# The price list of a work planner: charging VectorE and ScalarE by the times that the profile shows for one instruction

## The chip, the core and the metric

The kernel runs on one core of a Trainium2 chip. A core has a matrix engine (TensorE, PE in the profile, whose weight loads are listed as PEld), a vector engine (VectorE, DVE), an engine for activation functions (ScalarE, ACT), a general engine that here only issues DMAs and clears memory (GpSimd, POOL), and a queue engine that issues DMAs (SyncE, SP). Each has its own instruction stream and waits for the others by semaphores. SBUF is the on-chip memory, PSUM the accumulators that TensorE writes; a kernel keeps its data in tiles of 128 partitions, and tiles of one tag share a fixed number of buffers.

The metric is the device time of one execution in microseconds, as the median over runs.

## The reference

One layer of a diffusion backbone. `x` holds 256 latent tokens of width 2048, `ctx` 256 context tokens; everything is float32.

```python
sh1_x, sc1_x, g1_x, sh2_x, sc2_x, g2_x = adaln(c, w_mod, b_mod)       # silu(c) @ w_mod + b_mod, six parts; the same for c_ctx
hx = rmsnorm(x, norm1_g) * (1 + sc1_x) + sh1_x                         # hc from ctx in the same way
zx = hx @ w_in + b_in;  zc = hc @ w_in + b_in
s5 = s5_mixer(zc[:, 0:512], zx[:, 0:512], ...)          # diagonal complex state space, 32 groups x 64 states, both directions
cv = conv_module(zx[:, 512:1536], ...)                  # gate, depthwise convolution of 31 taps, layer norm, silu
ml = mlstm_mixer(zc, zx, ml_norm_g)                     # 4 heads of 256, both directions, chunkwise linear attention
x = x + g1_x * (concat([s5, cv, ml]) @ w_out)
x = x + g2_x * swiglu(rmsnorm(x, norm2_g) * (1 + sc2_x) + sh2_x, w_ffn_in, w_ffn_out)   # hidden width 5632
return rmsnorm(x, norm_f_g)
```

## The kernel before, in words

**The weight stream.** All large weight matrices are cut into 128x128 tiles and packed by `tile_order()` into one stream of 386 chunks of 8 tiles (`wst`), in the order in which they are used. A chunk is loaded by one DMA of 512 KB on SyncE's queue (`raw`, three buffers), rounded to the short float32 format on ScalarE (`whi`, line 201, `acopy`), and the rest `raw - whi` is taken on VectorE (`wlo`, line 168, `tt`). Every product is then formed from two or three matmuls of these parts. `nxt()` hands out the next weight tile; at the first tile of a chunk it starts the load and the split of a chunk ahead, and then calls `sc.pump()`.

**The stages**, in the order in which their weights lie in the stream: the first sixteen rows of tiles, with part of the K projection and the S5 input (chunks 0 to 13); the convolution's input (14 to 29); the rest of K (30 to 39); V (40 to 55); Q (56 to 71); the output gate O (72 to 87); the S5 gate GLU (88, 89); the first half of the output projection (90 to 105), which needs the convolution and S5; its second half (106 to 121), which needs the attention; and the feed-forward network (122 to 385), in four blocks.

**Side jobs.** Everything that is no weight matmul of these stages is written as a Python generator that yields between short pieces, and is registered with a planner, `Sched`, under a priority (lower goes first): `gates_job` (1), `mod_job` (2), `conv_job` and `s5_job` (3), `attention` (4). `mod_job` computes the four later parts of the modulation vector: the first (q = 0) by matmuls on TensorE, the others (q = 1, 2, 3) as sixteen steps a block of 512 columns, one on ScalarE and fifteen `scalar_tensor_tensor` on VectorE (`macc`, 128x512), followed by four transposes; four blocks make a q, eight loads `wm` of 512 KB a block come through GpSimd's queue with four buffers, and a step of four such instructions asks to be called again 10,000 units of TensorE time later (6,400 while on TensorE). `s5_job` works through 16 pairs of state groups; `prep` of the next pair runs beside `main5` of this one, and copies and a split (`gT`, `gs`) end it. `conv_job` takes the four channel tiles as their inputs come (`cdone`), 31 `scalar_tensor_tensor` each (`XB`, 128x256), then a layer norm. `attention` is registered at the start of stage Q and does the four heads one after the other; `qh` has one buffer, the state tiles `RH` one for each direction.

**The account.** `Sched` keeps three running sums in nanoseconds, `pe`, `dve` and `act`. Each helper that issues an instruction adds its price: `mm` (line 203) adds for a matmul of n columns `max(n, 256) / 2.36` (four times that for full float32), the helpers at lines 167 to 200 add for VectorE and ScalarE. These sums are Python numbers; they set only in which order instructions are emitted. `pump()` is called once a chunk and lets in pieces of ready jobs, the lowest priority number first and the earliest due among equals, until an engine's sum is more than `AHEAD` before TensorE's:

```python
def pump(self):
    self.dve = max(self.dve, self.pe - LAG)
    self.act = max(self.act, self.pe - LAG)
    for _ in range(400):
        if self.dve > self.pe + AHEAD or self.act > self.pe + AHEAD:
            return
        ready = [j for j in self.jobs if j[2] <= self.pe]
```

with `AHEAD, LAG = 3500.0, 500.0`. Where a later stage needs a job's result, `finish(j)` (or `need_mod(q)`) emits all that is left of it at once, without the pump: `conv_job` and `gates_job` at the start of V (lines 1019, 1020), `s5_job` and `attention` after O, ahead of GLU, `readout` and `need_mod(2)` between the halves of the output projection (the feed-forward input is scaled by these vectors, `A2` and `mods[:, 1]`).

The framework below then gives each engine its instructions in about this order of emission; where the inputs of an instruction are late in its own plan of times, it can put a later one first.

Of the kernel before, what the change touches and what calls it, by code (L numbers as in the profile page):

```python
# [36 lines left out]
MOD_PACE_D = 5000.0  # L37
P_CONV, P_S5, P_MOD, P_ATT, P_GATE = (3, 3, 2, 4, 1)
AHEAD, LAG = 3500.0, 500.0
PUMP_EVERY = 8  # L40
S5_Y = (3000, 0, 0, 0)
ATT_Y = (200, 1200, 3000)
# [108 lines left out]
def hybrid_layer_kernel(ctx: ExitStack, tc: tile.TileContext, xt, ctxt, wm1, wmr, wst, wg, bvrow, pvd, cstd, s5p, out):  # L151
# [6 lines left out]
    sc = Sched()  # L158


    def n_of(ap):
        n = 1
        for s in ap.shape[1:]:
            n *= s
        return n

    def tt(o, a, b, op):
        V.tensor_tensor(out=o, in0=a, in1=b, op=op)  # L168
        sc.dve += 62 + 1.05 * n_of(o)

    def ts(o, a, s1, op0, s2=None, op1=None):
        if op1 is None:
            V.tensor_scalar(o, a, s1, None, op0=op0)
        else:
            V.tensor_scalar(o, a, s1, s2, op0=op0, op1=op1)
        sc.dve += 62 + 0.6 * n_of(o)

    def stt(o, a, s, b, op0, op1):
        V.scalar_tensor_tensor(o, a, s, b, op0=op0, op1=op1)  # L179
        sc.dve += 62 + 1.05 * n_of(o)  # L180

    def vcopy(o, a):
        V.tensor_copy(o, a)
        sc.dve += 62 + 0.8 * n_of(o)

    def rsum(o, a):
        V.tensor_reduce(out=o, in_=a, op=OP.add, axis=mybir.AxisListType.X)
        sc.dve += 62 + 1.05 * n_of(a)

    def scan(o, d0, d1, init, op0, op1):  # L190
        V.tensor_tensor_scan(o, d0, d1, init, op0=op0, op1=op1)  # L191
        sc.dve += 62 + 1.05 * n_of(o)

    def act(o, a, f, bias=0.0, scale=1.0, pin=False):
        i = S.activation(o, a, f, bias=bias, scale=scale)  # L195
        if pin:
            tc.keep_in_program_order(i)
        sc.act += 190 + 0.84 * n_of(o)

    def acopy(o, a):  # L200
        S.copy(o, a)  # L201
# [61 lines left out]
    def split(c):  # L263
        his[c] = sb.tile([128, CH * 128], F32R, name="whi", tag="whi", bufs=3)
        acopy(his[c], raw[c])
        los[c] = sb.tile([128, CH * 128], F32R, name="wlo", tag="wlo", bufs=3)
        tt(los[c], raw[c], his[c], OP.subtract)
        for d in (raw, his, los):
            d.pop(c - 4, None)
# [6 lines left out]
    def split_to(c):  # L276
        while st["split"] <= min(c, NCH - 1):
            split(st["split"])
            st["split"] += 1

    def nxt(n=1):
# [3 lines left out]
        if i == 0:  # L285
# [4 lines left out]
            else:  # L290
                fetch_to(c + RAW_LA)
                split_to(c + SPL_LA)
        if i % PUMP_EVERY == 0:
            sc.pump()
# [18 lines left out]
    def rsqrt(o, ps, n, scale, eps, epsv):  # L313

        y, t = tmp(n), tmp(n)
        act(y, ps, AF.Ln, bias=eps, scale=scale)
        act(y, y, AF.Exp, scale=-0.5)
        stt(t, y, -0.5 * scale, y, OP.mult, OP.mult)
        stt(t, ps, epsv / scale, t, OP.add, OP.mult)
        stt(o, t, 1.5, y, OP.add, OP.mult)  # L320
# [28 lines left out]
    def load_gates():  # L349
        wgr = tmp(256).rearrange("p (k n) -> p k n", k=KT)  # L350
        nc.sync.dma_start(wgr, wg)
        acopy(wgs[:, :, 0:16], wgr)
        tt(wgs[:, :, 16:32], wgr, wgs[:, :, 0:16], OP.subtract)
# [22 lines left out]
    cs = sb.tile([128, KT, 32], F32, name="cs")  # L376
    V.memset(cs, 0.0)
    act(cs[:, :, 0], pvc("c", 0, 16), AF.Silu)
    act(cs[:, :, 1], pvc("cc", 0, 16), AF.Silu)
    b1sc = sb.tile([128, 16], F32, name="b1sc")  # L380
    ts(b1sc, pvc("bm", 16, 16), 1.0, OP.add)

    hx = sb.tile([128, KT, 2, NT], F32R, name="hx", tag="hx")
# [14 lines left out]
    def matvec_end(ft):  # L398
        ps = mvp.pop(ft)
        e = tmp(256)  # L400
        acopy(e, ps[:, 0:256])
        for i in range(2):
            P.transpose(ps[:, 256 + 128 * i:384 + 128 * i], e[:, 128 * i:128 * i + 128], ident)
        sc.pe += 220
        a = sb.tile([128, 4], F32, name="as1", tag="as1", bufs=4)
        rsum(a.rearrange("p (q r) -> p q r", q=2), ps[:, 256:512].rearrange("p (q j r) -> p q r j", q=2, j=4)[:, :, 0:2, :])
        ts(a[:, 0:2], a[:, 0:2], pvc("bm", ft), OP.add)
        ts(a[:, 2:4], a[:, 2:4], b1sc[:, ft:ft + 1], OP.add, pvc("n1g", ft), OP.mult)
        AS[ft] = a
# [3 lines left out]
    for half, src in ((0, xr), (1, cr)):  # L413
        for q in range(4):
            sq, s2 = tmp(), tmp()
            for i, t in ((0, sq), (1, s2)):
                act(t, src[:, 4 * q + 2 * i:4 * q + 2 * i + 2, :].rearrange("p k n -> p (k n)"), AF.Square)
            tt(sq, sq, s2, OP.add)
            for i in range(2):
                mm(stp[:, half * 256:half * 256 + 256], ones, sq[:, 256 * i:256 * i + 256], q + i == 0, q + i == 4,  # L420
                   native=True)
# [303 lines left out]
    def mod_job():  # L725
      for q in range(4):
        while mst["go"] < q:
            yield 500
        for b in range(4):
# [27 lines left out]
            if on_pe:  # L757
                rsum(dst, ps.rearrange("p (f j r) -> p f j r", f=4, j=4)[:, :, :, 0])
            else:
                for j in range(4):  # L760
                    S.activation(acc[:, 128 * j:128 * j + 128], ps[:, 128 * j:128 * j + 128], AF.Copy,
                                    accum_out=dst[:, j:j + 1])
                    sc.act += 390
# [15 lines left out]
    def s5_moves():  # L779
        for s in range(4):  # L780
            for q in range(4):
                o = U[32 * s:32 * s + 32, q::4, :]
                i = zT[32 * q:32 * q + 32, :, s::4]
                if (s + q) % 2:
                    vcopy(o, i)
                else:
                    acopy(o, i)

    def s5_job():
# [71 lines left out]
        def main5(p):  # L861
# [17 lines left out]
            for d in range(2):  # L879
                for ri in range(2):  # L880
                    scan(Vr[:, d, ri, :], rho[:, u0 + d:u0 + d + 1].to_broadcast([128, 128]), Vr[:, d, ri, :],
                         0.0, OP.mult, OP.add)
# [33 lines left out]
        for hh in range(2):  # L916
            for j in range(4):
                for q in range(4):
                    o, i = gT[hh][32 * q:32 * q + 32, :, j::4], U[32 * j:32 * j + 32, q + 8 * hh:q + 8 * hh + 5:4, 64:128]
                    if (j + q) % 2:  # L920
                        vcopy(o, i)
                    else:
                        acopy(o, i)
                yield
# [26 lines left out]
    def gates_job():  # L951
# [23 lines left out]
        for c in range(2):  # L975
            sl = slice(256 * c, 256 * c + 256)
            scan(b[0:32, sl], o1, f[0:32, sl], 0.0, OP.mult, OP.add)
            scan(b[32:64, sl][:, ::-1], o2, f[32:64, sl][:, ::-1], 0.0, OP.mult, OP.add)
# [447 lines left out]
```

## Time and profile before

| | |
|---|---|
| median of 3 runs | 1460.43 us (1458.61 to 1460.6) |
| the profiled execution, as timed | 1461.92 us |
| its span from the first to the last instruction | 1460.2 us |
| TensorE busy | 1416.0 us (97% of the span) |
| VectorE busy | 1058.8 us (73%) |
| ScalarE busy | 740.4 us (51%) |
| mean granted TensorE clock | 0.990 |

How to read it: a group of instructions has its line, engine, operation, the tile it writes and those it reads, and the shapes; "L168" is a helper's line, so the same line stands for many uses and the tile's name tells them apart. "mean ns of one" is the time from an instruction's start to its end, as recorded. The busy time of an engine counts stretches in which two recorded instructions overlap once. A row of waits gives the sum, how many there were, and the longest.

The stages lie in the span, by the first matmul that uses their weights, at 157.9 (after the convolution's first two chunks), 329.4 (V), 442.5 (Q), 582.1 (GLU), 640.3 (second half of the output projection) and 696.7 us (feed-forward network).

### The profile page before, as it was taken

To read this page: it belongs to the slowest core of one execution; us is meant where nothing else is said; L and a number is where in the kernel's file an instruction comes from. 1 tells how busy PE (TensorE), PEld (TensorE's weight loads), DVE (VectorE), ACT (ScalarE), POOL (GpSimd) and SP (SyncE) were. 2 spreads that over 40 slices of the span, in tenths; PEclk is the share of its full clock that TensorE was granted. 3 is DMA by queue.
4 is the path that set the end of the run, shared out by engine and by line. 5 is a ranking of instruction groups with operands and counts; after the bars stand their busy time and mean duration, and the time that the engine had idled before them with its cause. 6 is when DMAs were issued, how large, how long until landed. Compare 5 with 4: busy or idle time off the path is not lost.

```text
span 1460.2 us, 25526 instructions
## 1 busy us (share of the span) xinstructions
PE 1416.0 (97%) x9856; PEld 1242.3 (85%) x9856; DVE 1058.8 (73%) x2104; ACT 740.4 (51%) x1279; POOL 107.3 (7%) x207
## 2 busy tenths in 40 slices
PE   6999899999999999999999999999999999999996
PEld 3888787887878999898998888888888888888885
DVE  7655699998988887888877778566555665556665
ACT  4334786654656555645555545433444334444353
POOL 1221111110001010011000010000000000000000
PEclk9999999999999999999999999999999999999998
DMA  9998464443436666689478787555555555555553
GB/s 365 359 359 300 156 234 142 164 165 117 143 120 226 219 238 236 243 310 343 145 234 278 277 299 240 187 189 186 189 188 187 187 188 188 188 188 188 188 177 112
DMA packets 87929, 315.31 MB, mean 216 GB/s; under 512 B 10096, under 2 KB 10880, under 8 KB 87808
## 3 DMA queue, kind: packets, MB, share of 16 engines
q1 hardware_dynamic: 60912, 216.67, 43.4%
q0 software_dynamic: 26896, 97.02, 18.8%
q8 instruction: 77, 1.26, 0.3%
q14 instruction: 44, 0.36, 0.1%
HBM read 311.55 MB, written 2.10 MB: 215 GB/s over the span
## 4 chain that ended last, share of the span: by engine, by line
PE 87%; DVE 5%; ACT 3%; DMA 2%; issue 1%; SPq 0%; DVEq 0%; ACTq 0%
PE ps_m L208 55%; PE ps_qk L208 20%; PE ps_b L208 12%; DMA raw<-in_wst_dram 1%; DVE tmp L168 1%; ACT whi L201 1%; DVE macc L179 1%; DVE wlo L168 1%; DMA tmp<-in_wg_dram 1%; ACT tmp L195 1%; PE ps_b L845 0%; ACT U L201 0%; PE ps_b L755 0%; DVE tmp L191 0%; DVE tmp L179 0%
## 5 line engine op out<-in xcount | busy, mean ns | idle before, releaser
L168 DVE TENSOR_TENSOR wlo<-raw,whi 128x1024 fp32r<-128x1024 f32 x386 | 471.3, 1222 | 268.0 <-ACT whi L201 264.4
L201 ACT CAST whi<-raw 128x1024 fp32r<-128x1024 f32 x386 | 403.8, 1047 | 478.8 <-PE ps_m L208 240.6
L208 PE MATMUL ps_m<-h,whi 128*128 128x512 f32 (+1 forms) x800 | 251.9, 369 | 3.5 <-ACT h L195 3.5
L208 PE MATMUL ps_m<-ffa,whi 128*128 128x512 f32 x704 | 248.8, 395 | 0.0
L208 PE MATMUL ps_qk<-h,whi 128*128 128x512 f32 (+1 forms) x688 | 233.2, 383 | 0.0
L208 PE MATMUL ps_m<-h,wlo 128*128 128x256 f32 x704 | 199.6, 284 | 0.0
L208 PE MATMUL ps_m<-ffa,wlo 128*128 128x256 f32 x704 | 198.9, 283 | 0.0
L208 PE MATMUL ps_m<-hx,whi 128*128 128x256 f32 x960 | 187.2, 291 | 5.5 <-ACT hx L195 3.6
L208 PE MATMUL ps_qk<-h,wlo 128*128 128x256 f32 x656 | 185.5, 283 | 0.0
L208 PEld LDWEIGHTS ps_m<-h,whi 128*128 128x128 f32 x800 | 144.9, 190 | 30.2 <-ACT h L195 4.0
L208 PEld LDWEIGHTS ps_m<-hx,whi 128*128 128x128 f32 x960 | 149.1, 190 | 24.7 <-issue 16.3
L208 PEld LDWEIGHTS ps_m<-ffa,whi 128*128 128x128 f32 x704 | 132.2, 188 | 32.2 <-issue 1.2
L208 PEld LDWEIGHTS ps_qk<-h,whi 128*128 128x128 f32 x688 | 127.2, 188 | 27.1
L179 DVE SCALAR_TENSOR_TENSOR macc<-wm,cs,macc 128x512 f32<-128x512 f32 x180 | 134.1, 745 | 6.2 <-ACT macc L195 3.8
L208 PE MATMUL ps_m<-hx,wlo 128*128 128x256 f32 x480 | 136.0, 284 | 0.0
L208 PEld LDWEIGHTS ps_m<-h,wlo 128*128 128x128 f32 x704 | 133.1, 189 | 0.0
L208 PEld LDWEIGHTS ps_m<-ffa,wlo 128*128 128x128 f32 x704 | 132.3, 188 | 0.1
L208 PEld LDWEIGHTS ps_qk<-h,wlo 128*128 128x128 f32 x656 | 123.3, 188 | 0.0
L337 POOL DMA_DIRECT2D wm<-in_wmr_dram x128 | 67.5, 528 | 607.7 <-DVE macc L179 431.3
L179 DVE SCALAR_TENSOR_TENSOR xres<-ps_m,mods,xres 128x256 f32<-128x256 f32 x160 | 76.9, 481 | 36.4 <-PE ps_m L208 34.4
L208 PEld LDWEIGHTS ps_m<-hx,wlo 128*128 128x128 f32 x480 | 91.2, 190 | 0.7 <-DVE wlo L168 0.7
L168 DVE TENSOR_TENSOR tmp<-tmp 128x256 f32<-128x256 f32 (+3 forms) x128 | 51.2, 410 | 6.1 <-ACT tmp L195 5.0
(268 smaller groups left out, 2135.7 us busy)
## 6 DMA issues: line engine op xcount, KB each, us to landing
raw<-in_wst_dram SPq DMA_DIRECT2D x386, 512.0 KB, 3.8
wm<-in_wmr_dram POOLq DMA_DIRECT2D x128, 512.0 KB, 5.3
wm<-in_wm_dram POOLq DMA_DIRECT2D x32, 512.0 KB, 7.0
wmu<-in_wm_dram POOLq DMA_DIRECT2D x16, 512.0 KB, 7.0
wmt<-in_wm_dram POOLq DMA_DIRECT2D x7, 512.0 KB, 5.8
wm<-in_wm_dram SPq DMA_DIRECT2D x5, 512.0 KB, 10.3
xr<-in_xt_dram SPq DMA_DIRECT2D x4, 512.0 KB, 6.0
cr<-in_ctxt_dram SPq DMA_DIRECT2D x4, 512.0 KB, 9.0
```

The source lines that it names most:

```text
L168: V.tensor_tensor(out=o, in0=a, in1=b, op=op)
L179: V.scalar_tensor_tensor(o, a, s, b, op0=op0, op1=op1)
L195: i = S.activation(o, a, f, bias=bias, scale=scale)
L201: S.copy(o, a)
L208: i = P.matmul(o, lhsT=l, rhs=r, start=start, stop=stop, skip_group_check=sgc, **kw)
L337: i = (q or nc.gpsimd).dma_start(wm[key], src)
```

## The change

The prices that `tt`, `ts`, `stt`, `vcopy`, `rsum` and `scan` add for an instruction on VectorE, and `act` for one on ScalarE, become others. The fixed part on VectorE goes from 62 to 148 ns (`DVE0`); the part for each element goes from 0.6 to 1.02 for `ts`, from 0.8 to 0.92 for `vcopy`, from 1.05 to 2.05 for `scan`, and stays at 1.05 for the others; `act` adds 100 ns where the bias is a tile. The prices of matmuls, `AHEAD`, `LAG` and the jobs' own waits stay. No instruction is added or removed.

```diff
@@ -37,6 +37,7 @@
 MOD_PACE_D = 5000.0
 P_CONV, P_S5, P_MOD, P_ATT, P_GATE = (3, 3, 2, 4, 1)
 AHEAD, LAG = 3500.0, 500.0
+DVE0 = 148
 PUMP_EVERY = 8
 S5_Y = (3000, 0, 0, 0)
 ATT_Y = (200, 1200, 3000)
@@ -166,36 +167,36 @@
 
     def tt(o, a, b, op):
         V.tensor_tensor(out=o, in0=a, in1=b, op=op)
-        sc.dve += 62 + 1.05 * n_of(o)
+        sc.dve += DVE0 + 1.05 * n_of(o)
 
     def ts(o, a, s1, op0, s2=None, op1=None):
         if op1 is None:
             V.tensor_scalar(o, a, s1, None, op0=op0)
         else:
             V.tensor_scalar(o, a, s1, s2, op0=op0, op1=op1)
-        sc.dve += 62 + 0.6 * n_of(o)
+        sc.dve += DVE0 + 1.02 * n_of(o)
 
     def stt(o, a, s, b, op0, op1):
         V.scalar_tensor_tensor(o, a, s, b, op0=op0, op1=op1)
-        sc.dve += 62 + 1.05 * n_of(o)
+        sc.dve += DVE0 + 1.05 * n_of(o)
 
     def vcopy(o, a):
         V.tensor_copy(o, a)
-        sc.dve += 62 + 0.8 * n_of(o)
+        sc.dve += DVE0 + 0.92 * n_of(o)
 
     def rsum(o, a):
         V.tensor_reduce(out=o, in_=a, op=OP.add, axis=mybir.AxisListType.X)
-        sc.dve += 62 + 1.05 * n_of(a)
+        sc.dve += DVE0 + 1.05 * n_of(a)
 
     def scan(o, d0, d1, init, op0, op1):
         V.tensor_tensor_scan(o, d0, d1, init, op0=op0, op1=op1)
-        sc.dve += 62 + 1.05 * n_of(o)
+        sc.dve += DVE0 + 2.05 * n_of(o)
 
     def act(o, a, f, bias=0.0, scale=1.0, pin=False):
         i = S.activation(o, a, f, bias=bias, scale=scale)
         if pin:
             tc.keep_in_program_order(i)
-        sc.act += 190 + 0.84 * n_of(o)
+        sc.act += 190 + 0.84 * n_of(o) + (100 if not isinstance(bias, float) else 0)
 
     def acopy(o, a):
         S.copy(o, a)
```

## Rows read from the trace of the kernel before

**Rows 1.** The page's parts 1 (busy time) and 4 (chain by engine).
```profile
PE 1416.0 (97%) x9856; PEld 1242.3 (85%) x9856; DVE 1058.8 (73%) x2104; ACT 740.4 (51%) x1279; POOL 107.3 (7%) x207
...
PE 87%; DVE 5%; ACT 3%; DMA 2%; issue 1%; SPq 0%; DVEq 0%; ACTq 0%
```

**Rows 2.** Waits of TensorE, 157 to 640: us in total, times, longest.
```profile
PE ps_m L208 <- ACT whi L201: 1.7, 1, 1.7
PE ps_b L998 <- DVE rows L168: 1.4, 1, 1.4
...
PE ps_m L208 <- DVE wlo L168: 0.6, 1, 0.6
PE ps_b L208 <- DVE tmp L168: 0.5, 2, 0.3
```

**Rows 3.** Busy time by stretch; behind the engines the clock, DMA share, GB/s.
```profile
157.90:329.40 171.50, 168.93 (x1608) 144.83 (x1608) 159.09 (x436) 115.11 (x251) 21.10 (x40) 0.98 0.51 175
329.40:442.50 113.10, 112.59 (x690) 89.58 (x689) 97.75 (x242) 62.54 (x140) 8.51 (x16) 1.00 0.40 133
442.50:582.10 139.60, 137.89 (x974) 129.05 (x973) 113.12 (x257) 77.40 (x150) 13.74 (x26) 0.99 0.66 226
582.10:640.30 58.20, 54.92 (x459) 53.84 (x457) 49.02 (x78) 29.93 (x47) 5.28 (x10) 1.00 0.78 275
640.30:696.70 56.40, 51.85 (x429) 48.99 (x426) 49.68 (x74) 30.09 (x64) 8.45 (x16) 1.00 0.90 321
```

**Rows 4.** Groups on VectorE by shape, 157.9 to 582.1.
```profile
L168 DVE TENSOR_TENSOR wlo<-raw,whi 128x1024 fp32r<-128x1024 f32 x74 | 90.0, 1219 | 24.4 <-ACT whi L201 24.1
L179 DVE SCALAR_TENSOR_TENSOR XB<-XB,pv 128x256 f32<-128x256 f32 x120 | 53.6, 477 | 0.6
L179 DVE SCALAR_TENSOR_TENSOR macc<-wm,cs,macc 128x512 f32<-128x512 f32 x72 | 53.6, 744 | 3.6 <-ACT macc L195 3.1
L191 DVE TENSOR_TENSOR_SCAN Vr<-s5c,Vr 128x128 f32<-128x128 f32 x64 | 23.3, 405 | 0.0
```

**Rows 5.** VectorE in order of time: start, us, line, operation, tiles.
```profile
329.72 1.04 DVE L191 TENSOR_TENSOR_SCAN Vr<-s5c,Vr 128x128 f32<-128x128 f32 x3
330.69 0.87 DVE L168 TENSOR_TENSOR tmp<-LW,bb 128x128 f32<-128x128 f32 x4
...
577.88 1.22 DVE L168 TENSOR_TENSOR wlo<-raw,whi 128x1024 fp32r<-128x1024 f32 x1
579.01 2.32 DVE L179 SCALAR_TENSOR_TENSOR macc<-wm,cs,macc 128x512 f32<-128x512 f32 x3
...
697.47 0.42 DVE L168 TENSOR_TENSOR tmp<-xres,rs 128x256 f32<-128x256 f32 x1
697.80 0.41 DVE L168 TENSOR_TENSOR h<-tmp,h 128x256 fp32r<-128x256 f32 x1
```

**Rows 6.** The same stretches for tile macc alone: PE, PEld, DVE, ACT.
```profile
329.40:442.50 113.10, 1.31 (x8) 0.83 (x8) 17.12 (x23) 2.58 (x10) 1.00 0.40 133
442.50:582.10 139.60, 1.80 (x12) 1.46 (x12) 36.45 (x49) 5.58 (x27) 0.99 0.66 226
582.10:640.30 58.20, 0.97 (x8) 0.92 (x8) 13.38 (x18) 1.86 (x9) 1.00 0.78 275
640.30:696.70 56.40, 1.43 (x11) 0.96 (x8) 22.30 (x30) 4.87 (x26) 1.00 0.90 321
```

**Rows 7.** Tile RH (attention) by stretch; the last steps of heads three and four.
```profile
442.50:582.10 139.60, 40.79 (x176) 32.58 (x176) 19.67 (x56) 20.07 (x55) 0.99 0.66 226
...
542.00 0.74 DVE L175 TENSOR_SCALAR RH<-qh,mvv,tmp 128x256 f32<-128x256 f32 x2
...
563.63 0.73 DVE L175 TENSOR_SCALAR RH<-qh,mvv,tmp 128x256 f32<-128x256 f32 x2
```

**Rows 8.** The chain of waits into the feed-forward network: start, us, what.
```profile
687.78 0.44 PE ps_b L755 x4
...
688.85 0.87 ACT macc L761 x7
...
696.07 0.61 ACT h L195
```

## The prediction

> **What bounds the kernel now.** I read the page first: TensorE is busy for 97% of the span and makes up 87% of the chain of waits [rows 1]. Next, the waits of TensorE in the stretch where side work runs: on VectorE they come to 1.4 + 0.6 + 0.5 = 2.5 us, and the largest other one here is 1.7 [rows 2]. Then the stretches one by one: from 157.9 to 582.1 TensorE is busy for 168.93 + 112.59 + 137.89 = 419 of 424 us, VectorE for 159.09 + 97.75 + 113.12 = 370 [rows 3]. So in the convolution and K stages VectorE is nearly full (93%), but the weight splits come out in time. TensorE is the bound, and the order of emission leaves it some 5 us of idle time here. A new order can win little; it can lose whatever it makes TensorE wait for.
>
> **Are the new prices truer?** They are the recorded durations: 1219, 477, 744 and 405 ns [rows 4] against new prices of 1223, 417, 686 and 410, and old ones of 1137, 331, 600 and 196. But an engine is occupied from one start to the next. Three scans begin at 329.72 and the next operation at 330.69, so a scan takes 0.32 us, not 0.41; a split at 577.88 is followed at 579.01, after 1.13, not 1.22; a 256-column operation at 697.47 is followed at 697.80, after 0.33, not 0.42 [rows 5]. Each lasts about 85 ns longer than it occupies the engine. The old price is right for splits and 256-column operations, too low for a scan (196 against 320); the new one, with those 85 ns taken off the durations, is too high for all four, by 25 to 90 ns.
>
> The rows decide this. The Trainium skill, "Perfetto Trace Analysis", section Optimizing Scalar/DVE Operations, says the same: some 60 ns of overhead occupy VectorE, and the profiled latency is about twice that because the second half overlaps the next instruction. The Trainium skill, "VectorE: DVE Perf Modes", section The DRAIN you can't avoid, says that the next operation does not start until the pipe is empty; by that rule the new prices would be the right ones. The starts in rows 5 speak against it here.
>
> **The change, part by part.** No instruction is added; all that moves is when the pump stops. I compare the sums of the account from the start of the convolution stage to the end of O.
>
> TensorE's sum. A 256-column matmul counts 256/2.36 = 108 ns. Weights: convolution 128 tiles x 3, K 80 x 6, V 16 chunks of 5.2 us, Q and O 256 x 3, together 41.6 + 52.1 + 83.3 + 83.3 = 260 us. Side matmuls: gates 8.4, modulation q = 0 15-16, S5 16 pairs x 3.2, attention 4 heads x 10, and small ones: about 119. Together 379, for 424 us of real time: a ratio of 0.89.
>
> VectorE's sum, old: 74 splits x 1.137 = 84; S5 116 (7.04 a pair, and its final copies); convolution 46 (124 taps x 0.331, and its norm); attention 27; gates 5; modulation 43 (72 instructions x 0.6 [rows 4]); small ones 9. Together 330, against 370 us really busy: 0.89 again. The two sums drift from reality alike, so the old account, wrong in its parts, lets in about what fits.
>
> VectorE's sum, new: splits 74 x 1.223 = 90.5; S5 165 (9.96 a pair: four scans at 0.41 for 0.196, the other two dozen instructions 86 ns more each, and the copies); convolution 58; attention 39 (9.8 a head); gates 9; modulation 49; small ones 10. Together 421, where TensorE's 379 and AHEAD's 3.5 allow 383. So some 38 us are not let in by GLU, although VectorE would have time for them. ScalarE's 100 ns more come to under 10 us and do not stop the pump.
>
> Who is left out follows from the priorities. *Convolution and K*: the weights and fixed side matmuls make 113 us plus 0.49 for each us of S5 (old price). Before, S5 got 78 and the convolution 29 of old price here. With VectorE's new sums and the same 0.37 : 1 between them, 1.41x + 1.26 (0.37x) + 43 for splits and gates + 9 lost at bursts = 113 + 0.49x, so x = 45 and the convolution gets 17. *V*: `finish` emits what is left of the convolution, some 72 taps where it was 37, which puts the account 36 us ahead; at 5.2 - 1.2 us a chunk the pump stays shut for 8 of V's 16 chunks. S5 then gets about 27 more. *Q and O*: 83 us of weights, 39 of splits, 22 of modulation leave S5 another 27. About 17 of its 116 (nearly two pairs and the final copies) and, since attention has the last priority, all four heads are left at the end of O and are emitted in a row ahead of GLU.
>
> **Step 1, the heads in a row.** Their matmuls occupy TensorE for 40.8 us [rows 7] wherever they stand. Spread out, a head took 563.63 - 542.00 = 21.6 us, filled with weight matmuls [rows 7]. In a row no weights of O are left to fill the gaps: GLU needs S5's copies, and the output projection's second operand `mixs` takes the buffer of `vx`, which the last head frees. From below the chain hides wholly behind its own matmuls: 0. From above four heads follow each other at 21.6: 86 - 41 = +46. I take the middle, +22, because the next head's first matmuls can run during this one's norm but `qh` has one buffer.
>
> **Step 2, the modulation.** Its steps ask for a turn every 10 us, but get none while the pump is shut (8 chunks of V; after the heads, which put VectorE some 15 us ahead, most of the 18 chunks to 640.3). Before, 23 + 49 + 18 of the 120 instructions of q = 1 and 2 were done by 640.3, and 30 came after [rows 6]. I count 12 steps fewer, at 3 instructions a step 36, with the rest of a block up to 40. They are emitted by `need_mod(2)` and needed by the feed-forward input; today's chain there already ends with the last block's transposes and ScalarE sums [rows 8]. No cover is left: VectorE is busy for 49.7 of 56.4 us there and the DMA engines at 0.90 with 321 GB/s [rows 3]. On VectorE 40 x 0.66 (0.744 less 0.085) = 26 us; by DMA 40/15 blocks x 8 loads x 0.524 MB = 11 MB, at 321 GB/s 35 us, beside it. From below, 20, if the idle 6.7 us take some; from above 35. I take +28. GpSimd's queue holds nothing else; SyncE's weight loads share the DMA engines and are in these 0.90.
>
> **Step 3, the taps at V's start.** 35 more taps of 0.4 us go in front of the second chunk's split. The same pile of 37 cost one wait of 0.6 us before [rows 2], since a V chunk takes 5.2 us or more and the splits slip in between chained taps. From below 0, from above 8 (14 us less one chunk and its lead); I take 0.
>
> **Step 4, the gain.** VectorE is less full through K, so the 2.5 us of waits on it go: -2.5; from above -6 with ScalarE's. A late split is next.
>
> Sum: 22 + 28 + 0 - 2.5 = +47.5. The profiled execution took 1461.9 us (span 1460.2 and 1.7 around it), so 1509.4 on its own time; it stands 1.5 above the median of 1460.43, so 1508 for the median.
>
> **Rivals.** *One pile only* (chance 0.20): the account's tail is softer than I sum, S5 ends within O and most heads are let in, or the modulation catches up. Then one of the steps counts: 1460.4 + 22 or + 28 - 2.5, about 1480 to 1486. For it: 38 us of overcharge are only 10% of 383, and my stage sums carry some 10 us of error. Against: attention is last in the order, and what is cut off is cut off there.
> *Both at the upper bounds* (0.10): +46 + 35 + 8 - 2.5, about 1547.
> *Nothing measurable* (0.10): the framework fills idle engines from the piles ahead of their place, about 1460. For it: the taps before V were mixed in among splits; against: heads need TensorE, which is always busy with earlier work.
> *Faster* (0.10): the durations are the true occupation, so the old account overfilled VectorE, and the stricter one removes TensorE's waits, in K above all. It decides if the left-over at the end of O is nothing, that is if S5's new sum were some 129 rather than 165. Price: the waits of rows 2 with their neighbours, -6, about 1454. Against: the starts in rows 5, and 54 us of idle VectorE in a stretch that by durations would hold 370 + 935 x 0.085 = 449 of 424 us [rows 3]. The Trainium skill's rule of the pipe that must empty, named above, is the one that would make it so; no row here bears it out.
>
> **How the numbers follow.** Likeliest with 0.50: 1508, its own range 1488 to 1535. A measurement of this kernel tells 0.2% (2.9 us) from no change. Faster by more 0.10, within 0.10, slower 0.80 (0.50 + 0.20 + 0.10). The range leaves out the faster case and the top: 1457 to 1545.
>
> **What would show it.** Step 1: between the last matmul on O's weights and GLU's first a stretch of 60 us or so with RH's matmuls and hardly a weight matmul, TensorE idle for 15 us or more in it. The account: at V's start 28 or fewer of the 64 S5 scans done; VectorE under 80% busy in convolution and K. Step 2: about 70 macc instructions, not 30, behind the start of the projection's second half, and the feed-forward network starting late by as much. Wrong would be: heads spread through Q and O as before, an idle TensorE no larger than 44 us, or new waits on `wlo`.

## The result, and the profile after

The changed kernel takes 1571.37 us (median of 4 runs, 1568.92 to 1576.36) where the kernel before takes 1460.01 on the same chip: a ratio of 1.0769, with a 95% interval of 1.0740 to 1.0797. The direction was as predicted, and so were two of the three places in which time was lost. The size was not: +111 us, where +47.5 was forecast and +85 was the end of the range. Line numbers are one higher than before (L168 is now L169, L755 is L756).

The page of the changed kernel, parts 1 and 4, beside [rows 1]:

```profile
PE 1433.2 (91%) x9856; PEld 1255.9 (80%) x9856; DVE 1067.3 (68%) x2104; ACT 738.1 (47%) x1276; POOL 107.7 (7%) x207
...
PE 79%; DVE 9%; ACT 4%; DMA 4%; issue 3%; POOL 0%; SPq 0%; DVEq 0%; ACTq 0%; POOLq 0%
```

TensorE and VectorE have as many instructions as before, and VectorE's busy time grew by 8.5 us. TensorE's share of the chain fell from 87% to 79%; VectorE, ScalarE, the DMAs and "issue" took it over. So work is not added but stands in other places, uncovered (nothing on TensorE runs beside it). The waits of TensorE, whole span, tell which work (total, times, longest); the first three are not in [rows 2] or are 0.5 there:

```profile
PE ps_b L756 <- DVE macc L180: 42.5, 4, 15.0
PE ps_b L209 <- DVE tmp L169: 21.1, 4, 9.7
PE ps_b L209 <- DVE RH L169: 16.9, 7, 5.7
PE ps_qk L209 <- DVE tmp L169: 10.6, 4, 8.7
PE ps_m L209 <- ACT whi L202: 5.1, 3, 2.2
...
PE ps_m L209 <- DVE wlo L169: 1.2, 2, 0.6
```

`macc` is the modulation, `tmp` into `ps_b` is S5's chain, `RH` is the heads. The fourth row was there before (10.1 us in the kernel before, outside the stretch of [rows 2]). The fifth, for the first part of a weight split, was 1.7 and lies in the feed-forward network now. Waits on `wlo` stay small: 1.7 us in all, where they were 0.8. The stages of after, cut at the same first matmuls as [rows 3], except that O ends at 520.7 with its weights and the first pile reaches to the output projection's first matmul (columns: busy time of PE, PEld, DVE, ACT and POOL, granted clock, DMA share, GB/s):

```profile
157.10:302.60 145.50, 142.26 (x1253) 126.81 (x1253) 133.07 (x326) 77.68 (x152) 14.81 (x28) 0.97 0.53 181
302.60:416.40 113.80, 113.75 (x710) 89.37 (x706) 70.40 (x169) 54.94 (x117) 9.03 (x17) 1.00 0.41 138
416.40:520.70 104.30, 102.80 (x941) 101.57 (x939) 88.84 (x172) 59.06 (x122) 12.24 (x23) 1.00 0.73 256
520.70:647.00 126.30, 79.78 (x419) 63.81 (x419) 73.02 (x260) 65.97 (x145) 0.54 (x1) 0.75 0.09 30
647.00:693.30 46.30, 46.30 (x393) 46.30 (x391) 30.28 (x42) 19.49 (x23) 0.00 (x0) 0.99 0.53 172
693.30:744.40 51.10, 50.85 (x427) 48.58 (x426) 48.69 (x74) 28.85 (x61) 8.49 (x16) 1.00 0.86 310
744.40:795.50 51.10, 5.31 (x25) 3.33 (x23) 37.68 (x58) 8.82 (x36) 12.72 (x24) 0.56 0.81 284
```

Read it as a ledger. V starts at 302.6 instead of 329.4, Q at 416.4 instead of 442.5, and O's weights are through at 520.7: TensorE is ahead because side work was not let in. Then come 126.3 us in which GLU's are the only matmuls on weights (30 GB/s), TensorE idle for 46.5 of them: the first pile, S5's rest and four heads. The second half of the projection starts at 693.3 instead of 640.3, net **+53.0**. It takes 102.2 us instead of 56.4, **+45.8**: in the last 51.1 of them TensorE works for 5.3. The third loss lies in the feed-forward network, between its start and the first matmul of its second block: 323.3 us instead of 313.5, **+10**. Together +109, and the span grew by 108.5.

What stands in the two piles: tile `macc` in three stretches (PE, PEld, DVE, ACT), beside [rows 6]; the S5 and gate scans (line 192, L191 before) on VectorE, first before up to V's start, then after up to V's start and in the pile; tile `RH`, beside [rows 7]:

```profile
520.70:693.30 172.60, 0.00 (x0) 0.00 (x0) 0.00 (x0) 0.00 (x0) 0.81 0.21 68
693.30:744.40 51.10, 1.88 (x12) 1.27 (x12) 22.31 (x30) 4.43 (x23) 1.00 0.86 310
744.40:795.50 51.10, 3.32 (x12) 2.15 (x12) 33.78 (x45) 6.07 (x31) 0.56 0.81 284
```

```profile
157.90:329.40 171.50, 20.46 (x49) 0.98 0.51 175
...
157.10:302.60 145.50, 12.98 (x28) 0.97 0.53 181
...
520.70:575.90 55.20, 4.29 (x12) 0.60 0.07 21
```

```profile
520.70:575.90 55.20, 4.98 (x18) 3.39 (x18) 1.19 (x4) 3.06 (x4) 0.60 0.07 21
575.90:647.00 71.10, 43.42 (x164) 33.05 (x164) 18.33 (x52) 12.48 (x38) 0.86 0.11 37
```

75 `macc` instructions follow the second half's start, where 30 did. Of S5's 64 scans 20 are done by V's start (8 of the 28 belong to the gates), where 41 were (49 less the same 8); 12, three pairs' worth, are still to come at 520.7, where none was. The first pile thus has two parts: 55 us of S5's chain and its copies, in which the first head only begins, and 71 us of heads. The chain of waits within the first part (start, us, what):

```profile
546.50 0.67 DVE Vr L169 x2
547.82 0.96 DVE Vr L192 x3
548.79 2.24 DVE tmp L169 x9
551.17 1.96 PE ps_b L209 x8
554.58 3.53 PE ps_b L209 x23
558.20 0.69 DVE Vr L169
```

That is one pair, from VectorE's products through the scans to TensorE and back; the same operation `Vr` of line 169 starts a pair at 545.08 and at 558.20, so a pair takes 13.1 us when no weight matmul stands between.

### The profile page after: what moved, and what is told of

Same layout as the page of the kernel before. It is cut to its first block, busy times and chain, and to the rows that moved or that the text cites. A ratio compares the mean times of both kernels' runs of the same rounds, so it can differ in the third digit from the quotient of the medians.

```text
span 1568.7 us, 25548 instructions
## 1 busy us (share of the span) xinstructions
PE 1433.2 (91%) x9856; PEld 1255.9 (80%) x9856; DVE 1067.3 (68%) x2104; ACT 738.1 (47%) x1276; POOL 107.7 (7%) x207
## 4 chain that ended last, share of the span: by engine, by line
PE 79%; DVE 9%; ACT 4%; DMA 4%; issue 3%; POOL 0%; SPq 0%; DVEq 0%; ACTq 0%; POOLq 0%
PE ps_m L209 50%; PE ps_qk L209 18%; PE ps_b L209 10%; DMA raw<-in_wst_dram 2%; DVE macc L180 1%; DVE tmp L169 1%; DVE XB L180 1%; DVE wlo L169 1%; ACT L196 1%; DMA wm<-in_wmr_dram 1%; ACT tmp L196 1%; ACT whi L202 1%; DMA tmp<-in_wg_dram 1%; ACT U L202 0%; ACT gT L202 0%
## 5 line engine op out<-in xcount | busy, mean ns | idle before, releaser
L169 DVE TENSOR_TENSOR wlo<-raw,whi 128x1024 fp32r<-128x1024 f32 x386 | 471.8, 1223 | 308.3 <-ACT whi L202 304.7
L209 PE MATMUL ps_m<-hx,whi 128*128 128x256 f32 x960 | 183.9, 288 | 3.8 <-ACT hx L196 3.6
L169 DVE TENSOR_TENSOR tmp<-tmp 128x256 f32<-128x256 f32 (+3 forms) x128 | 51.6, 413 | 7.2 <-ACT tmp L196 5.4
```

The lines of the kernel that those rows point to most:

```text
L209: i = P.matmul(o, lhsT=l, rhs=r, start=start, stop=stop, skip_group_check=sgc, **kw)
```

## The experiments

All the programs issue the same instructions as the kernel before and differ in their order alone. "Old prices" means the kernel before with one edit; the others are edits of the changed kernel, unless they say otherwise. "Out" is the first matmul of the output projection, against 591.5 in the kernel before; "stage" the time of the projection's second half (56.4 before); `macc` the instructions of that tile in it.

**The heads late, old prices.** One line keeps the attention from being let in, so `finish` emits it ahead of GLU.

```diff
     aj = sc.add(attention(), P_ATT)
+    aj[2] = 1e12
```

> The old prices; only the four attention heads are withheld from the pump and emitted in one row ahead of GLU. Theory A (in the changed kernel both the heads and the rest of S5 cost, the heads the smaller part, because their own matmuls occupy TensorE for 40.8 of some 70 us): GLU starts late by 20 to 30 us and the modulation adds up to 8, about 1490. Theory B (the heads are the whole of the 53 us that the changed kernel lost by the output projection's start): about 1515. Theory C (a row of heads hides behind its own matmuls, and S5 was all of it): 1460 to 1468.

1503.22 us, ratio 1.0292 (1.0262 to 1.0322), between theories A and B. Out came 31.0 us later; the rest of the +42.5 came in the second half, where 45 `macc` stood instead of 30. So the heads in a row alone cost +31, inside step 1's 0 to +46, above its +22. TensorE's waits name the chain within a head:

```profile
PE ps_b L208 <- DVE RH L168: 14.7, 7, 4.1
PE ps_b L755 <- DVE macc L179: 11.5, 1, 11.5
```

**S5's last four pairs late, old prices.** In the S5 job:

```diff
             live = [b, a]
+            if p == 12:
+                yield 1e12
             while live:
```

> The old prices; only S5 is stopped at its 13th pair until GLU, so that some 44 pieces with 12 us of matmuls are emitted there, and the heads go on in Q and O. Theory A (chain of S5 pairs without cover): 56 us of chain less 12 us of matmuls, and up to 8 of modulation, about 1505. Theory B (heads are all): 1460 to 1470. Theory C (S5 is all): 1515.

1511.79 us, ratio 1.0351 (1.0321 to 1.0381), between theories A and C; out +40.5. Pairs that no weights cover cost more than the heads do, though their matmuls are under a third of the heads' (11.6 against 40.0 us in the planner's own price). The waits show S5's chain, `tmp` into `ps_b`, and its last split:

```profile
PE ps_b L208 <- DVE tmp L168: 25.2, 4, 8.0
PE ps_b L755 <- DVE macc L179: 11.1, 1, 11.1
PE ps_m L208 <- ACT gs L201: 7.6, 1, 7.6
```

**Both late, old prices.** The two edits above together.

> The old prices, with both put late by hand: the last four pairs of S5 and all four heads are emitted after O (44 S5 steps, 45 of the heads; 18 modulation steps in the second half). If step 1 of the changed kernel is nothing but these two piles, the second half starts 50 to 56 us later than in the kernel before, as it did with the new prices (+53), and the end comes near 1460 + 53 + 11 = 1524. If the two piles cost as much as each did alone (+31 and +40), the second half starts some 71 us later, and the end is about 1542. If the new prices do harm by something else too, both numbers stay well below these: under +45 and under 1515.

1532.35 us, ratio 1.0494 (1.0479 to 1.0508). Out +59.4, the second half's start +58.3 (changed kernel: +55.5 and +53.0). The first pile's loss is reproduced with the old prices, 4 to 5 us above, so nothing but the pile is needed for it. This pile is a little longer: 16 scans follow the last matmul on O's weights, 12 in the changed kernel, which had the products and scans of that pair done just before its pile begins at 520.7 and its first matmuls ready then:

```profile
515.07 0.69 DVE Vr L169
...
521.17 1.30 PE ps_b L209 x10
```

These 6 us of chain are about the difference. The parts, +31.0 and +40.5, do not add fully: the sum would be 71.5. The end, +71, is short of the changed kernel's +109 by what the modulation does: the second half took 12.6 us longer here, not 45.8.

**The modulation late, old prices.**

```diff
-MOD_PACE_D = 5000.0
+MOD_PACE_D = 10000.0
```

> The old prices; only the modulation's steps ask for a turn every 20,000 units in place of 10,000. S5 and the heads are let in on time, and 27 steps of the modulation are left for the second half of the projection, as in the changed kernel (28). Theory A (a block costs about 17 us of its own there, whatever came before): the feed-forward network starts 38 to 46 us later than in the kernel before, the end comes near 1500 to 1506. Theory B (the price of step 2 as predicted, 20 to 35 us for as many instructions; the rest of the changed kernel's loss comes from the first pile, which puts the loads late): 1480 to 1495.

1482.55 us, ratio 1.0155 (1.0138 to 1.0172). The second half took 84.4 us, +28.0. That looks like step 2's +28, and like theory B; but the rows of `macc` (columns as above, the second row is the second half) show that fewer instructions stood there than in the changed kernel:

```profile
578.00:633.50 55.50, 0.92 (x7) 0.88 (x8) 11.15 (x15) 1.86 (x9) 1.00 0.72 246
633.50:717.90 84.40, 3.71 (x19) 2.43 (x17) 44.79 (x60) 8.62 (x44) 0.82 0.89 310
```

One block of 15 was carried out ahead of its place, in the first half, where the changed kernel has none: in the planner's order of emission, which can be counted in the program, 75 of them are left for `need_mod(2)` here and 79 in the changed kernel. The two theories of this run part only if that is counted, and then all the programs fall on one line:

| `macc` in the second half | programs | stage, us |
|---|---|---|
| 1 | modulation paced faster | 56.5 |
| 11 | dearer matmuls (1.90) | 56.7 |
| 15 | no limit | 55.6 |
| 30 | before; fixed part at 62 | 56.4; 56.2 |
| 41 | occupied durations | 61.9 |
| 45 | heads, S5, both late; 105; 2.10; modulation let in when full | 67.6 to 71.6 |
| 60 | modulation late | 84.4 |
| 75 | fixed part alone; the changed kernel | 101.2; 102.2 |

The first 30 cost nothing, and from there each block of 15 costs 11 to 18 us. The programs with no pile ahead of it (41 and 60) lie on the same line as those with one.

**The account relaxed for the modulation alone, new prices.** `pump` may let in a modulation step also when an engine's sum is too far ahead.

```diff
-            if self.dve > self.pe + AHEAD or self.act > self.pe + AHEAD:
-                return
-            ready = [j for j in self.jobs if j[2] <= self.pe]
+            full = self.dve > self.pe + AHEAD or self.act > self.pe + AHEAD
+            ready = [j for j in self.jobs if j[2] <= self.pe and (not full or j[0] == P_MOD)]
```

> The changed kernel, but the modulation job is let in even where the account is full. Theory A (its 28 pieces at the second half of the projection and 15 in the feed-forward network cost 46 and 10 us because they were kept out): the wait ahead of the feed-forward network and the 10 us later go, while the row of S5 grows from 40 to 57 pieces: 1571 - 56 + 25 = 1540. Rival (the network starts late for another reason, such as weight loads or the clock): 1571 or more.

1543.02 us, ratio 1.0565 (1.0534 to 1.0595). The second half fell from 102.2 to 71.6 us and the third loss is gone (+82.9 at the feed-forward network's start, +82.4 at the end), but out rose to +70.1: S5 paid for the modulation's turns (20 of its scans follow O's weights, 12 in the changed kernel). Of the 41 us won in the second half and behind it, a third (14.6) went into the first pile: here the account decided how much was left over, the priority mostly whose.

**Which price does it.** Five programs with the new price list and one thing altered:

```diff
 # 1: the fixed part alone
-        sc.dve += DVE0 + 2.05 * n_of(o)
+        sc.dve += DVE0 + 1.05 * n_of(o)
...
 # 2: the parts for each element alone
-DVE0 = 148
+DVE0 = 62
...
 # 3: half of the fixed rise
+DVE0 = 105
...
 # 4, 5: dearer matmuls
-max(n, 256)) / 2.36 /
+max(n, 256)) / 2.10 /
+max(n, 256)) / 1.90 /
```

Program 1 takes back the slopes of `ts` and `vcopy` and ScalarE's 100 ns as well.

> Only the fixed part of the price is changed (148 for 62 ns), all slopes and ScalarE's price are the old ones. Theory (the 86 ns for each of a thousand instructions are the overcharge): 30 pieces of S5, four heads and 27 of the modulation are left, so 1550, nearly all of the change's loss. Rival (the scans' slope, 410 for 196 ns, holds S5 back): 1490 or less.

> Only the slopes and ScalarE's 100 ns are changed, the fixed part is the old 62 ns. Theory A (the fixed part is the loss): 1455 to 1466. Rival (the scan's slope holds S5 back): over 1475.

> The changed kernel with half of the fixed rise (DVE0 = 105 in place of 148; 62 before). The account then leaves 44 steps of the heads, 3 of S5 and 18 of the modulation for their due places, and none for q = 3. Theory A (the time is what stands uncovered in the piles): heads +31 as when they alone were put late, nothing for S5, modulation +8 to 11: about 1497 to 1502. Theory B (the loss grows in proportion to the overcharge, wherever the work is let in): half of 111, about 1515.

> The changed kernel with the price of a matmul raised by 12% (2.36 to 2.10 columns a nanosecond), about its real pace in the stretch. Theory (the ratio of the two sums decides; S5 ends in time, but 37 of the heads' 45 pieces and 18 of the modulation are left): the heads' row costs some 25 and the modulation 8, about 1490. Rival (the new prices do harm in themselves): 1540 or more.

> All the new VectorE and ScalarE prices stay; only the price of a matmul rises by 24% (divided by 1.90 in place of 2.36), so that TensorE's sum grows as theirs did. Nothing of S5 or the heads is then left at the end of O, 5 steps of the modulation in the second half. Theory A (the loss is the ratio of the sums, not any single price): 1452 to 1466. Theory B (a price too high for scans, or the spacing by which single pieces are let in, costs of itself): 1480 or more. The jobs that wait for a turn by TensorE's sum come 24% sooner, which theory A takes to be worth a few us either way.

Measured: (1) 1555.81, ratio 1.0652 (1.0621 to 1.0683). (2) 1464.59, 1.0029 (1.0019 to 1.0039). (3) 1500.07, 1.0277 (1.0261 to 1.0293). (4) 1495.23, 1.0237 (1.0199 to 1.0275). (5) 1466.15, 1.0044 (1.0032 to 1.0056). The 86 ns on every VectorE instruction do most of it, 95 of the 111 us. The other prices, the scans at double among them, cost 4 us alone and 16 on top of the 86 ns. Half of the 86 costs 40 of the 111 us, as theory A of that run had it: the heads are late (out +28.7), S5 is not, and 45 `macc` are left. And with all the new prices kept, 24% on the matmuls takes away 105 of the 111. Its waits, whole span, are those of the kernel before again:

```profile
PE ps_qk L209 <- DVE tmp L169: 10.8, 5, 8.6
PE ps_b L209 <- ACT whi L202: 4.0, 1, 4.0
...
PE ps_b L756 <- DVE macc L180: 0.5, 1, 0.5
```

So the new prices do no harm in themselves; the ratio of VectorE's sum to TensorE's does.

**Prices by occupied time.** The fixed part back to 62, the scan at 2.0 for each element, `scalar_tensor_tensor` 64 ns dearer where its scalar is a tile:

```diff
-DVE0 = 148
+DVE0 = 62
...
-        sc.dve += DVE0 + 1.05 * n_of(o)
+        sc.dve += DVE0 + (1.05 if isinstance(s, float) else 1.05 + 64.0 / max(n_of(o), 64)) * n_of(o)
```

> Prices as the starts of consecutive instructions show them: 62 ns fixed, 1.02 for ts, 0.92 for copies, 2.0 for scans, 64 ns more where a scalar comes from a tile. Theory A (what matters is that the sum of prices fits the sum of TensorE; 15 pieces of modulation left, 14 before): 1455 to 1466. Rival (any price above the old one costs): slower in proportion, 1475 or more.

1477.77 us, ratio 1.0118 (1.0096 to 1.0140): theory A missed, and the time is the rival's. Prices nearer to the starts in [rows 5] are worse than the old ones. The dearer matmuls above speak against the rival's reason; what fits both is that TensorE's sum, at 0.89 of real time, was not raised with them. 41 `macc` are left, and out is 6.5 us late.

**No limit.** The new prices with `AHEAD` at 1e9, so that a ready job is always let in:

```diff
-AHEAD, LAG = 3500.0, 500.0
+AHEAD, LAG = 1e9, 500.0
```

> The changed kernel with the limit out of reach: the pump lets in whatever is due, the prices stand but nothing reads them. Theory A (the prices act through the limit alone, and VectorE has room for all side work in time): within 1% of the kernel before, 1450 to 1470, with no row of heads. Rival B (the limit protects the weight splits: without it VectorE's queue is long and splits come late): slower than before by over 2%, 1490 or more, with waits of TensorE on wlo.

1580.38 us, ratio 1.0814 (1.0784 to 1.0845). Theory A fell. Theory B's time came, but not for the reason that it gave: waits on `wlo` are 3.4 us in all. TensorE's longest new waits are for S5 and the convolution themselves, and all in the convolution and K stages (V starts at 477.6, 148 us later than in the kernel before), with the clock at 0.77 over 220 us (the row by stretch has the columns of the stages above):

```profile
PE ps_b L209 <- ACT Wb L202: 50.0, 8, 6.6
PE ps_b L209 <- DVE XB L180: 19.3, 3, 18.3
```

```profile
165.00:385.00 220.00, 154.55 (x1336) 122.73 (x1335) 154.42 (x489) 116.64 (x312) 19.61 (x37) 0.77 0.30 98
```

The reading is that, emitted too early, a chain's matmuls stand in TensorE's queue ahead of weights that could run, as emitted too late no weights are left. No run shows it by itself: in the 40 us around the longest wait (385 to 425) VectorE is busy for all 40.0, so a split might have come late there too. What is shown is the price: no limit costs about as much as one that is too tight.

**A try at better than both.** The kernel before with its modulation paced faster, so that next to nothing of it is left in the second half:

```diff
-MOD_PACE_D = 5000.0
+MOD_PACE_D = 3500.0
```

> The kernel before with its old prices; only the modulation's steps ask for a turn every 7,000 units in place of 10,000. In the second half 3 steps are then left in place of 14 (2.5 in place of 23 us of charge). If the chain into the feed-forward network was set by these, it starts up to 9 us sooner: 1451 to 1457. If TensorE's matmuls of the projection end there at the same time whatever the modulation does, or the earlier loads of the modulation's weights delay the stream in Q and O: 1458 to 1465.

1467.08 us, ratio 1.0048 (1.0035 to 1.0060), above both ranges. One `macc` was left there and the stage took 56.5 us all the same; Q, O and GLU started 6 to 10 us later. The 30 of the kernel before were free. None of the programs beats it.

## Why the prediction was right or wrong

**What bounds, and the account.** Right in kind: the old prices suit each other, and the new ones leave work over in the order of the priorities. The sums predicted 17 of S5's 116 units left at O's end, nearly two pairs and the copies; the trace has 12 scans left, three pairs, and the copies. They also had all four heads left, and the first head's matmuls indeed begin in the pile (18 of `RH` by 575.9, none before). "28 or fewer S5 scans at V's start" held, with 20. "VectorE under 80% busy in convolution and K" failed: 133.07 of 145.5, or 91%. The pump did let in fewer taps: in the order of emission 55 `scalar_tensor_tensor` of 256 columns come ahead of V, where it was 89, as the prediction's sums had it. But the framework put the pile's taps into the gaps, ahead of their place. Tile `XB` in that stage, before and after:

```profile
157.90:329.40 171.50, 1.67 (x6) 0.44 (x6) 44.73 (x102) 0.00 (x0) 0.00 (x0) 0.98 0.51 175
```

```profile
157.10:302.60 145.50, 1.70 (x10) 0.45 (x10) 55.30 (x128) 0.00 (x0) 0.00 (x0) 0.97 0.53 181
```

102 operations before, 128 after. This is the rival "the framework fills idle engines from the piles", true for work that needs VectorE alone and has its inputs; it did not save the S5 pairs and the heads, which need TensorE in turns.

One reading of [rows 5] was too wide. That an operation lasts 85 ns longer than it occupies the engine holds for the three kinds compared there, but not for `macc` after `macc`, where each reads the one before. Three in a row last 2.32 us in the same rows, so they start (2.32 - 0.74)/2 = 0.79 us apart, behind the recorded end of the one before; for them the new price of 686 ns is too low, not too high.

**Step 1 failed: a term was missing.** It names S5's rest as left over and then prices only the heads, at +22. The heads alone cost +31.0, within its bounds. S5's rest, priced at nothing, is a chain of 13.1 us a pair with no weight matmul beside it; the last four pairs alone cost +40.5, and both together +59.4 with the old prices. The changed kernel shows +53.0 net at the second half's start. Of the +33.5 between that and the predicted 22 + 0 - 2.5, 9 belong to the heads and some 24 to S5; the runs show the sum better than the split, since the parts overlap.

**Step 2 was right in its count and short in its price.** About 70 `macc` were forecast, 75 came. 40 more were priced at 28 us, or 10.5 a block of 15, with 35 as the upper bound; 45 more cost 45.8, or 15.3 a block, and the last three took 17 each. The chain into the feed-forward network, beside [rows 8], and the group of `macc` in the last 51.1 us show what the price left out:

```profile
783.24 5.59 DMA wm<-in_wmr_dram
...
788.93 0.76 DVE macc L180
789.72 0.76 DVE macc L180
...
792.10 1.13 PE ps_b L756 x4
...
793.25 1.15 ACT macc L762 x8
...
794.83 0.61 ACT h L196
```

```profile
L180 DVE SCALAR_TENSOR_TENSOR macc<-wm,cs,macc 128x512 f32<-128x512 f32 x45 | 33.8, 751 | 5.3 <-DMA wm<-in_wmr_dram 3.0 <-ACT macc L196 1.2
```

Each `macc` reads the one before, and they follow each other after 0.79 us, not 0.66: fifteen take 11.8 us, not 9.9. Behind them stand four transposes and ScalarE's sums, 2.3 us, and then the next block's first product on ScalarE, 0.75 us, which cannot start earlier since `macc` has one buffer. A load that comes late adds about 1 us a block (3.0 in three blocks, 1.3 in the last). Together these are the 16.1 us from the last but one block's transposes to the last one's. So the step that failed is the sum for a block: it took VectorE's busy time, or the loads beside it, and left out the spacing of dependent operations and the work of two other engines at a block's end. VectorE's time and the load's time do stand beside each other, but for that 1 us. That a block has this price whatever came before is what the table above shows. The prediction's "no cover is left" was wrong at the other end: 30 of these instructions cost nothing.

**Not named: the third pile.** The q = 3 part falls due in the feed-forward network and lost turns too: 42 of its 60 `macc` are left for that place in the order of emission, where none was before. It costs +10 us, which were gone when the modulation alone was let in (+82.9 at the network's start, +82.4 at the end). TensorE is idle for 6.4 us between 795.5 and 1118.8, 5.1 of them in the waits on `whi` above and 1.2 in two on `wlo`; the rest is spread over its busy time, and its cause was not sought. From 1050 to 1085, where 4.9 of the 6.4 us lie, VectorE and the DMA engines are both nearly full (columns as above):

```profile
1050.00:1085.00 35.00, 30.09 (x165) 24.74 (x164) 32.65 (x51) 12.57 (x20) 6.39 (x13) 1.00 0.94 336
```

**Step 3** came out at its 0, but its reason was hardly tested: most taps were done by then, so the pile that it prices hardly stood there (8 `XB` operations in V, 34 before). Its evidence was misread, too: the wait of 0.6 us on `wlo` in [rows 2] lies at 603, in the output projection, not at V's start. **Step 4**, -2.5, did not come: from 157 to the end of O's weights TensorE is idle for 4.8 us before [rows 3] and for 4.8 after, and waits on `rows` are 2.6 us where they were 2.2.

**The rivals.** "Faster", by durations that are true occupation, fell: the left-over at O's end was larger than predicted, not nothing, and when the ratio of the sums was put back (1466.15) nothing was gained over the kernel before either. "Both at the upper bounds", 1547, was nearest, and not for its reasons: it is 15 us too high for the heads and 8 for the taps, and short of S5's 24, of 11 for the modulation and of the third pile's 10.

What the prediction should have done: give each item of its own list of left-overs a term, priced as a chain without cover, and make the upper end of the range the sum of these chains. With the prices that the runs gave, that is four heads +46, two pairs at 13 us +26, three blocks at 17 us +51: +123, on the other side of the measured +111. The 46 was in the prediction; the 13 and the 17 were known only afterwards.

## What to carry to other kernels

An account that decides when side work is let in needs sums that drift alike, not prices that are each true: if one engine's price is raised by a tenth, raise the others' too, and count what is left at each due place before measuring the time. Whether a limit raised in proportion would do as well was not tried; none at all does not. Work left for a due place costs its whole chain, from engine to engine and back, not its busy time; price it by the spacing of its steps where nothing stands beside it, and give every left-over its own term. Here the framework pulled forward work of one engine (the convolution's taps), and not work that goes back and forth between two (S5's pairs, the heads).

## What was not expected of the hardware

The mean granted clock falls within the piles: 0.60 in the 55 us of S5's rest, in which TensorE worked for 25 us, 0.86 in the 71 us of the heads, in which it worked for 55, and 0.56 in the last 51 us of the modulation, in which it worked for 5.3. That is near the lower of its two levels (1.2 GHz; 1.00 is 2.4) in the first and the last. It was 0.99 to 1.00 in these stages before [rows 3]. The matmuls on `RH` took 48.40 us (182 of them), where they took 40.79 (176) [rows 7]: 266 ns each for 232, so in the pile the heads' own matmuls are dearer by about 6 us. In the modulation's pile the loads (24, beside two of the weight stream) moved 284 GB/s, less than the 321 beside the weight stream [rows 3]. The DMA engines are not the limit there (0.81 busy): the loads wait for a buffer, which `macc` gives back. GpSimd, which issues them, stood waiting for `macc` for 34.0 of the 51.1 us, and `macc` for the loads for 3.0.
